# Adding one block of the weights to another by accumulating DMAs, with one more seven-multiplication row pair in fourteen of the MLP products

## The chip, the cores and the metric

The kernel runs on one core of one Trainium2 chip. The metric is the device time of one execution in microseconds (us); lower is better. Everything is float32 in and float32 out. Engines are named as in the profile: PE (TensorE, matmuls), DVE (VectorE), ACT (ScalarE), POOL (GpSimd) and SP (the queue that issues the weight loads).

## The reference

A decoder trunk of two layers over 256 tokens of width 2048. Layer 0 is a retention layer, layer 1 a latent attention (MLA) layer, and behind each stands an MLP with a squared ReLU. Nearly all of the work is in products of a 256-row activation with large weights:

```python
D_MODEL, SEQ, D_FF = 2048, 256, 4 * 2048

def sq_relu_mlp(h, w1, w2):
    return jnp.square(jax.nn.relu(h @ w1)) @ w2

for layer in range(2):
    if layer == 0:
        x = x + retention(rms_norm(x, norm_mix[0]), ret_w_in[0], ret_w_out[0], cos, sin)
    else:
        k_nope, k_pe, v = mla_shared_kv(rms_norm(x, kv_norm_in), ...)
        x = x + mla_attention(rms_norm(x, norm_mix[1]), ..., k_nope, k_pe, v, ...)
    x = x + sq_relu_mlp(rms_norm(x, norm_mlp[layer]), mlp_w1[layer], mlp_w2[layer])
```

`retention` is a projection (queries, keys, values, gate), a decayed causal attention per head, and an output projection; the MLP is two products of 256 x 2048 x 8192.

## The kernel before, in words

**One product.** Float32 accuracy is reached by splitting both factors into a high and a low part (`fp32r`). ACT casts the weights' high part (L185), DVE subtracts it to get the low part (L186), and each product of blocks is three matmuls: high by high (L356), high by low (L357), low by high (L358).

**Row pairs and column pairs.** `gemm_pair` (L333) computes 1024 columns of a product, one *pair*. It goes through the weights in *row pairs* of 256 rows. A row pair is one load of 1 MB (L285) into a tile `raw` of 128 x 2048, whose four blocks of 128 x 512 lie in the order B11, B12, B22, B21. `quad` (L282) works off one row pair. It comes in two kinds:

- An *eight* does the four block products of each of two token halves: 8 products, 24 matmuls of 512 columns. DVE has two splits of 1024 columns.
- A *seven* uses the Strassen-Winograd scheme: 7 products, 21 matmuls, on sums of activations (`more`, made by `with_sums`, L392) and sums of weights. Before the change, DVE makes the weights' sums by one addition of 1024 columns (L321, B12 added to B11 and B22 at once) and two of 512 (L324, L325). Its splits are 1024, 512, 1024 and 1024 columns. The products that need no sums come first, three of them or nine matmuls; then those on the third split (columns `b[:, 0:2]`), then those on the fourth.

Each pair has eight row pairs, numbered 0 to 7. Lists say which of them are sevens: `THREE = (3, 5, 7)`, `FOUR = (1, 3, 5, 7)`, and `HEAD = (2, 4, 6, 7)` for the retention part. In a pair with sevens there are further accumulators (`p1`, `p5`, `p6`, `p7`), which `pair_out` (L368) copies and combines into four pairs of partial results.

**Buffers.** `raw` has four buffers, the split halves `wh` and `wl` have five each. SP can load row pair k only when the last split of row pair k - 4 has read its buffer. ACT can cast only into a `wh` that PE has finished with. So the loads run about three row pairs ahead of DVE, and DVE runs less than a row pair ahead of PE.

**The MLP.** `mlp` (L784) goes in four groups of 2048 hidden columns. In a group there are two pairs of the first product, called u0 to u7 over the four groups, and two pairs of the second product, called d0 and d1 in each group. What follows a pair is done by ACT, DVE and PE while the row pairs of the next one run:

- after a u pair: `pair_out`, `summed` (L387), ReLU (L797), transposes on PE (L205), square (L806), the split of four tiles `hid`, and `with_sums` for those of them that a seven will use (L396 to L398, and the split of `hid_more`);
- after a d pair: `pair_out`, and `to_home` (L145), which adds eight 256 KB blocks to x in HBM by accumulating DMAs on POOL's queue (L150), two to each of four places, so that the second must wait for the first.

The last group's d pairs add to x in SBUF: `x_tiles` (L133) brings x back from HBM (L140), and `into_next` (L467) adds, stores and transposes it.

**Order.** Each engine runs its instructions in the order that a scheduler wrote when the kernel was built. `later`, `tick` and `need` decide where follow-up work enters; the scheduler then reorders by its own estimates. At run time only semaphores hold an instruction back, and POOL's accumulating DMAs are issued in POOL's order: one that waits holds up those behind it.

Of the kernel before, what the change touches and what calls it, by code (L numbers as in the profile page):

```python
# [11 lines left out]
F32 = mybir.dt.float32  # L12
# [4 lines left out]
ALU = mybir.AluOpType  # L17
# [3 lines left out]
P = 128  # L21
NT = 2
# [21 lines left out]
NB = 4  # L44
# [2 lines left out]
NOPE, ROPE, MV, KVR, QR = 128, 64, 128, 512, 1536  # L47
KV_NBS, Q_NB = (320, 256), 384
GROUPS = (4, 4, 4, 4)
THREE, FOUR, HEAD = (3, 5, 7), (1, 3, 5, 7), (2, 4, 6, 7)  # L50
PI = math.pi

G_MIX0, G_MLP0, G_KV, G_MIX1, G_MLP1 = 0, 16, 32, 48, 64
# [15 lines left out]
def yoco(ctx: ExitStack, tc: tile.TileContext, a):  # L69
    nc = tc.nc  # L70
# [20 lines left out]
    def act_tile(name, dtype=F32R):  # L91

        return pool.tile([P, 2, 2, S], dtype, tag="act", bufs=24, name=name)
# [8 lines left out]
    def run_first():  # L102
        i = min(range(len(queue)), key=lambda i: queue[i][:2])
        due, _, fn = queue.pop(i)
        fn()
# [6 lines left out]
    def need(items, n):  # L112
        while len(items) < n:
            run_first()
# [14 lines left out]
    dram = ctx.enter_context(tc.tile_pool(name="dr", bufs=1, space=bass.MemoryType.DRAM))  # L129
    x_home = [[dram.tile([P, 512], F32, name=f"xh_{t}_{b}") for b in range(NB)] for t in range(NT)]  # L130
    x = [[None] * NB for t in range(NT)]

    def x_tiles(name):  # L133


        def bring(b):
            both = act_tile(f"x_{name}{b}", F32)
            for t in range(NT):
                x[t][b] = both[:, t].rearrange("p i s -> p (i s)")
                nc.gpsimd.dma_start(x[t][b], x_home[t][b])  # L140

        for b in range(NB):
            later(2 * b, lambda b=b: bring(b))

    def to_home(c, p):  # L145

        for j in range(2):
            for t in range(NT):
                for part in c[t][j]:
                    nc.gpsimd.dma_start(x_home[t][2 * p + j], part, accum_op=ALU.add)  # L150

    def into_x(done, c, p):
        for j in range(2):
# [125 lines left out]

            stream(w, chunk0 + g, 2048, f"{name}{g}", use, (lambda: done(acc)) if g == n - 1 else None)  # L280

    def quad(w, chunk, x, mm, name):  # L282

        raw = pool.tile([P, 2048], F32, tag="raw", bufs=4, name=f"{name}_raw")
        nc.sync.dma_start(raw, w[chunk])  # L285
        v, more = x

        def a(t, k):
            return [v[:, k, i, t * P : (t + 1) * P] for i in range(2)]

        def s(n):
            return [more[:, n // 2, i, n % 2 * P : (n % 2 + 1) * P] for i in range(2)]

        b = raw.rearrange("p (i n) -> p i n", i=4)

        def parts(src, part):
            n = src.free_size() // 512
            wh, wl = (
                pool.tile([P, 2, 512], F32R, tag=f"w{i}", bufs=5, name=f"{name}_w{i}{part}")[:, :n] for i in "hl"
            )  # L300
            split(wh, wl, src)
            return [[i[:, j] for i in (wh, wl)] for j in range(n)]

        b11, b22 = parts(b[:, 0:3:2], 0)
        if more is None:
            mm("c11", a(0, 0), b11)
            mm("c21", a(1, 0), b11)
            mm("c12", a(0, 1), b22)
            mm("c22", a(1, 1), b22)
            b12, b21 = parts(b[:, 1:4:2], 1)  # L310
            mm("c12", a(0, 0), b12)
            mm("c22", a(1, 0), b12)
            mm("c11", a(0, 1), b21)
            mm("c21", a(1, 1), b21)
            return
        mm("p1", a(0, 0), b11)
        mm("c12", s(3), b22)
        (b21,) = parts(b[:, 3:4], 1)
        mm("c11", a(0, 1), b21)

        nc.vector.tensor_tensor(  # L321
            b[:, 0:2], b[:, 0:3:2], b[:, 1].unsqueeze(1).to_broadcast([P, 2, 512]), op=ALU.add
        )
        nc.vector.tensor_tensor(b[:, 2], b[:, 0], b[:, 2], op=ALU.add)  # L324
        nc.vector.tensor_tensor(b[:, 3], b[:, 2], b[:, 3], op=ALU.add)  # L325
        u1, u3 = parts(b[:, 0:2], 2)
        mm("p5", s(1), u1)
        mm("p7", s(0), u3)
        u2, u4 = parts(b[:, 2:4], 3)
        mm("p6", s(2), u2)  # L330
        mm("c21", a(1, 1), u4)

    def gemm_pair(w, chunk0, act, kinds, name, done):  # L333

        made = {}
        total, count = {}, {}
        for seven in kinds:
            for key in ("c11", "c12", "c21"):
                total[key] = total.get(key, 0) + (1 if seven else 2)
            for key in ("p1", "p5", "p6", "p7") if seven else ("c22", "c22"):  # L340
                total[key] = total.get(key, 0) + 1

        def get(key):
            if key not in made:
                if key in ("p6", "p7"):
                    both = two_banks(f"{name}_p67")
                    made["p6"], made["p7"] = both[:, 0], both[:, 1]
                else:
                    made[key] = bank("tp" if key[0] == "p" else "acc", [512], f"{name}_{key}")
            return made[key]  # L350

        def mm(key, lhs, rhs):
            dst, n = get(key), count.get(key, 0)
            count[key] = n + 1
            (ah, al), (bh, bl) = lhs, rhs
            nc.tensor.matmul(dst, ah, bh, start=n == 0, stop=False)  # L356
            nc.tensor.matmul(dst, ah, bl, start=False, stop=False)  # L357
            nc.tensor.matmul(dst, al, bh, start=False, stop=n == total[key] - 1)  # L358

        for i in range(len(kinds)):  # L360
            need(act, i + 1)
            v, more = act[i]
            quad(w, chunk0 + i, (v, more if kinds[i] else None), mm, f"{name}{i}")
            if i == len(kinds) - 1:
                queue.append((clock[0] + 1, -1, lambda: pair_out(made, name, done)))
            tick()
# [374 lines left out]
    for h in range(RH):  # L741
        qk, gate, v, s = [], [], [], []
        if h == 0:

            def gated(acc, gate=gate):
# [16 lines left out]
                lambda acc, v=v, s=s, gate=gate: ret_valued(acc, 0, s, v, gate),  # L762
# [14 lines left out]
        kinds = HEAD if h > 1 else HEAD[1:]  # L777
# [6 lines left out]
    def mlp(layer, act, r, done):  # L784
        w1, w2 = a[f"mlp_w1_{layer}"], a[f"mlp_w2_{layer}"]
        f0 = 0
        for gi, nf in enumerate(GROUPS):
            hid, blocks = [], []
            last = gi == len(GROUPS) - 1

            def up(c, p, hid=hid, blocks=blocks, last=last):

                need(r, NT)
                c = summed(c)
                for t in range(NT):
                    for i in range(2):
                        nc.scalar.activation(c[t][i], c[t][i], AF.Relu, scale=r[t])  # L797

                def turn(i):
                    for q in (2 * i, 2 * i + 1):  # L800
                        name = f"hid{layer}_{p}{q}"
                        tp = transposed(
                            lambda t, j: c[t][q // 2][:, (q % 2 * 2 + j) * P : (q % 2 * 2 + j + 1) * P], f"{name}_tp"
                        )
                        u = f2k([2, S], f"{name}_u")
                        nc.scalar.activation(u, tp, AF.Square)  # L806
                        v = act_tile(name)
                        split_act(v, u)
                        blocks.append((v, with_sums(u, name) if len(blocks) in (THREE if last else FOUR) else None))
                        hid.append(v)  # L810

                later(0, lambda: turn(0))
                later(1, lambda: turn(1))

            for p in range(f0 // 2, (f0 + nf) // 2):
                kinds = THREE[not (p or layer) :] if p % 2 or not p else FOUR
                gemm_pair(
                    w1, p * 8, act, [i in kinds for i in range(8)], f"u{layer}_{p}", lambda c, p=p, up=up: up(c, p)
                )
            if last:  # L820
                x_tiles(f"mlp{layer}")
            for p in range(2):
                if last and p and layer:
                    for b in (2, 3):
                        need(hid, 2 * nf)
                        gemm(
                            a["mlp_w2t"], (b - 2) * nf, hid, 4 * nf, 512, f"d{layer}_{gi}{b}",
                            lambda acc, b=b: done(b, acc),
                        )
                    continue  # L830

                def add(c, p=p, last=last):
                    into_x(done, c, p) if last else to_home(c, p)

                kinds = [i in (FOUR if p and not last else THREE) for i in range(2 * nf)]
                gemm_pair(w2, p * 32 + 2 * f0, blocks, kinds, f"d{layer}_{gi}{p}", add)
            f0 += nf

# [347 lines left out]
```

## Time and profile before

| what | value |
|---|---|
| times of three runs | 2477.63, 2477.06, 2475.72 us (median 2477.06) |
| the profiled execution's own time | 2474.51 us |
| its span, first to last instruction | 2472.7 us |
| granted TensorE clock | 1.000 |
| PE busy | 2455.6 us (99%) |
| DVE busy | 2167.4 us (88%) |
| ACT busy | 1606.1 us (65%) |
| POOL busy | 251.6 us (10%) |
| DMA moved | 521.04 MB, mean 211 GB/s |

Instructions overlap with the next one on their engine: a matmul of 512 columns is shown as 0.39 us, but the next one starts 0.23 us later. So the rate of an engine is read from the starts of consecutive rows of the timeline, and not from the durations. In a timeline row the first number is the start in us from the beginning of the span, the second the duration; a bracket at the end names the idle time before it and who ended it, and no bracket means that the engine went straight on.

### The profile page before, as it was taken

Reading aid. Unit: us, or ns where it says so; the run is one execution under the profiler, and the core shown is the slowest. Engines: PE = TensorE matmul, PEld = TensorE weight load, DVE = VectorE, ACT = ScalarE, POOL = GpSimd, SP = SyncE. Lnnn points to the kernel's source line nnn. Section 1 sums busy time; section 2 is a strip of 40 time slices with the busy share of each in tenths; the row PEclk is TensorE's granted clock in tenths of the full one; section 3 lists DMA queues with packets and bytes.
Section 4 is the critical chain, followed back from the end, with each engine's and each line's share of the span. In section 5 each row is a group of like instructions: output and inputs, shape, how many; then the busy total and the mean of one; then the engine's idle time right before and its main releaser. Section 6 shows DMA issues by size and latency. Waiting matters only on the chain.

```text
span 2472.7 us, 31711 instructions
## 1 busy us (share of the span) xinstructions
PE 2455.6 (99%) x11635; PEld 2060.0 (83%) x11635; DVE 2167.4 (88%) x2805; ACT 1606.1 (65%) x2253; POOL 251.6 (10%) x310
## 2 busy tenths in 40 slices
PE   9999999999999999999999999999999999999999
PEld 7888888888888888888888888998888888888887
DVE  7799899889899999999999967776689999999996
ACT  6566656556676667667666766676566666676663
POOL 7300011000010010110110101110000201101100
PEclk9999999999999999999999999999999999999999
DMA  9555567555564685684785564445545856857854
GB/s 328 211 174 205 196 205 234 199 192 201 198 236 182 209 262 216 213 254 172 246 263 196 192 228 168 153 155 179 199 174 199 261 212 209 268 203 225 266 192 153
DMA packets 93403, 521.04 MB, mean 211 GB/s; under 512 B 11072, under 2 KB 12224, under 8 KB 40000
## 3 DMA queue, kind: packets, MB, share of 16 engines
q1 hardware_dynamic: 71856, 472.83, 53.8%
q0 software_dynamic: 21248, 46.15, 8.5%
q8 instruction: 91, 1.49, 0.2%
q14 instruction: 64, 0.52, 0.1%
q10 hardware_dynamic: 144, 0.05, 0.0%
HBM read 479.14 MB, written 39.85 MB: 210 GB/s over the span
## 4 chain that ended last, share of the span: by engine, by line
PE 91%; DVE 4%; ACT 3%; issue 1%; POOL 1%; DMA 0%; SPq 0%; ACTq 0%; POOLq 0%; DVEq 0%
PE u_c L358 7%; PE u_c L356 7%; PE u_c L357 7%; PE d_c L357 6%; PE d_c L358 6%; PE d_c L356 6%; PE rk_acc L274 2%; PE rq_acc L274 2%; PE rp_c L356 2%; PE rp_c L357 2%; PE rp_c L358 2%; PE u_p L358 2%; PE u_p L356 2%; PE u_p L357 2%; PE d_p L356 2%; PE d_p L358 2%
## 5 line engine op out<-in xcount | busy, mean ns | idle before, releaser
L185 ACT CAST u_wh<-u_raw 128x1024 fp32r<-128x1024 f32 x362 | 347.9, 991 | 207.8 <-DVE u_raw L321 100.8
L185 ACT CAST d_wh<-d_raw 128x1024 fp32r<-128x1024 f32 x358 | 344.1, 993 | 202.5 <-DVE d_raw L321 93.9
L186 DVE TENSOR_TENSOR u_wl<-u_raw,u_wh 128x1024 fp32r<-128x1024 f32 x362 | 402.0, 1144 | 47.2 <-ACT u_wh L185 41.7
L186 DVE TENSOR_TENSOR d_wl<-d_raw,d_wh 128x1024 fp32r<-128x1024 f32 x358 | 397.8, 1146 | 40.1 <-ACT d_wh L185 35.5
L356 PE MATMUL u_c<-u_wh,n 128*128 128x512 f32 x706 | 276.4, 392 | 0.0
L357 PE MATMUL u_c<-u_wl,n 128*128 128x512 f32 x706 | 275.5, 390 | 0.0
L358 PE MATMUL u_c<-u_wh,n 128*128 128x512 f32 x706 | 274.9, 389 | 0.0
L356 PE MATMUL d_c<-d_wh,hid 128*128 128x512 f32 x654 | 256.0, 392 | 0.0
L357 PE MATMUL d_c<-d_wl,hid 128*128 128x512 f32 x654 | 255.4, 391 | 0.0
L358 PE MATMUL d_c<-d_wh,hid 128*128 128x512 f32 x654 | 254.6, 389 | 0.0
L185 ACT CAST rp_wh<-rp_raw 128x1024 fp32r<-128x1024 f32 (+1 forms) x166 | 160.7, 982 | 140.9 <-DVE rp_raw L321 64.9
L186 DVE TENSOR_TENSOR rp_wl<-rp_raw,rp_wh 128x1024 fp32r<-128x1024 f32 (+1 forms) x166 | 184.9, 1137 | 26.7 <-ACT rp_wh L185 24.4
L358 PEld LDWEIGHTS u_c<-u_wh,n 128*128 128x128 f32 x706 | 132.6, 188 | 27.4
L356 PEld LDWEIGHTS u_c<-u_wh,n 128*128 128x128 f32 x706 | 132.6, 188 | 26.9
L357 PEld LDWEIGHTS u_c<-u_wl,n 128*128 128x128 f32 x706 | 132.6, 188 | 26.7
L358 PEld LDWEIGHTS d_c<-d_wh,hid 128*128 128x128 f32 x654 | 122.8, 188 | 25.4
L356 PEld LDWEIGHTS d_c<-d_wh,hid 128*128 128x128 f32 x654 | 122.8, 188 | 25.2
L357 PEld LDWEIGHTS d_c<-d_wl,hid 128*128 128x128 f32 x654 | 122.9, 188 | 24.7
L150 POOL DMA_DIRECT2D xh<-d_c x48 | 41.6, 867 | 856.6 <-ACT d_c L373 854.7
L185 ACT CAST ro_wh<-ro_raw 128x1024 fp32r<-128x1024 f32 x88 | 85.7, 997 | 59.7 <-DVE ro_raw L321 25.7
L356 PE MATMUL rp_c<-rp_wh,a 128*128 128x512 f32 x286 | 111.9, 391 | 0.0
L357 PE MATMUL rp_c<-rp_wl,a 128*128 128x512 f32 x286 | 111.4, 390 | 0.2 <-DVE rp_wl L186 0.2
(465 smaller groups left out, 6075.6 us busy)
## 6 DMA issues: line engine op xcount, KB each, us to landing
u_raw<-in_mlp_w SPq DMA_DIRECT2D x128, 1024.0 KB, 5.2
d_raw<-in_mlp_w SPq DMA_DIRECT2D x120, 1024.0 KB, 4.9
rp_raw<-in_ret_w_gv SPq DMA_DIRECT2D x56, 1024.0 KB, 4.9
ro_raw<-in_ret_w_out SPq DMA_DIRECT2D x32, 1024.0 KB, 4.9
uq_raw<-in_mla_w_uq SPq DMA_DIRECT2D x24, 768.0 KB, 4.1
rq_raw<-in_ret_w_qk SPq DMA_DIRECT2D x16, 1024.0 KB, 5.0
rk_raw<-in_ret_w_qk SPq DMA_DIRECT2D x16, 1024.0 KB, 4.8
wo_raw<-in_mla_w_o SPq DMA_DIRECT2D x16, 1024.0 KB, 4.8
```

What stands on the lines that cost most here:

```text
L150: nc.gpsimd.dma_start(x_home[t][2 * p + j], part, accum_op=ALU.add)
L185: nc.scalar.copy(h, src)
L186: nc.vector.tensor_tensor(l, src, h.bitcast(F32), op=ALU.subtract)
L274: nc.tensor.matmul(acc[f], wh[:, cols], a.rearrange("p i s -> p (i s)"), start=k == 0, stop=k == nk - 1)
L356: nc.tensor.matmul(dst, ah, bh, start=n == 0, stop=False)
L357: nc.tensor.matmul(dst, ah, bl, start=False, stop=False)
L358: nc.tensor.matmul(dst, al, bh, start=False, stop=n == total[key] - 1)
```

## The change

1. `quad` no longer loads. A new function `block` loads a row pair and, for a seven, issues a DMA on POOL's queue that adds B11 to B12 inside `raw` (SBUF to SBUF, accumulating). `gemm_pair` calls it two row pairs ahead, so the accumulating DMA of row pair k stands in POOL's program ahead of the work on row pair k - 2.
2. DVE's three additions are then all of 512 columns. U1 is B11 + B12, which the DMA has made in the place of B12.
3. `FOUR` becomes (2, 3, 5, 7), and it is used in all u pairs but the first, and in both d pairs of every group but the last. The pairs that had three sevens and now have four are u1, u3, u5, u7 in both layers and the d0 of three groups in both layers: fourteen pairs.
4. `to_home` has a second place in HBM, `more_home`, for the second part of each block. The first write of a round is a plain one, later ones accumulate. `x_tiles` adds that place to x by a further accumulating DMA per block.

```diff
-THREE, FOUR, HEAD = (3, 5, 7), (1, 3, 5, 7), (2, 4, 6, 7)
+THREE, FOUR, HEAD = (3, 5, 7), (2, 3, 5, 7), (2, 4, 6, 7)
...
                 nc.gpsimd.dma_start(x[t][b], x_home[t][b])
+            for t in range(NT):
+                if (t, b) in has_more:
+                    nc.gpsimd.dma_start(x[t][b], more_home[t][b], accum_op=ALU.add)
+                    has_more.remove((t, b))
...
-                for part in c[t][j]:
-                    nc.gpsimd.dma_start(x_home[t][2 * p + j], part, accum_op=ALU.add)
+                b = 2 * p + j
+                part, more = c[t][j]
+                nc.gpsimd.dma_start(x_home[t][b], part, accum_op=ALU.add)
+                if (t, b) in has_more:
+                    nc.gpsimd.dma_start(more_home[t][b], more, accum_op=ALU.add)
+                else:
+                    nc.gpsimd.dma_start(more_home[t][b], more)
+                    has_more.add((t, b))
...
-    def quad(w, chunk, x, mm, name):
+    def block(w, chunk, seven, name):
 
         raw = pool.tile([P, 2048], F32, tag="raw", bufs=4, name=f"{name}_raw")
         nc.sync.dma_start(raw, w[chunk])
+        if seven:
+            nc.gpsimd.dma_start(raw[:, 512:1024], raw[:, 0:512], accum_op=ALU.add)
+        return raw
+
+    def quad(raw, x, mm, name):
...
-        nc.vector.tensor_tensor(
-            b[:, 0:2], b[:, 0:3:2], b[:, 1].unsqueeze(1).to_broadcast([P, 2, 512]), op=ALU.add
-        )
-        nc.vector.tensor_tensor(b[:, 2], b[:, 0], b[:, 2], op=ALU.add)
+        nc.vector.tensor_tensor(b[:, 2], b[:, 1], b[:, 2], op=ALU.add)
+        nc.vector.tensor_tensor(b[:, 0], b[:, 2], b[:, 0], op=ALU.subtract)
         nc.vector.tensor_tensor(b[:, 3], b[:, 2], b[:, 3], op=ALU.add)
-        u1, u3 = parts(b[:, 0:2], 2)
+        u3, u1 = parts(b[:, 0:2], 2)
...
+        raws = []
         for i in range(len(kinds)):
+            for k in range(len(raws), min(i + 3, len(kinds))):
+                raws.append(block(w, chunk0 + k, kinds[k], f"{name}{k}"))
             need(act, i + 1)
             v, more = act[i]
-            quad(w, chunk0 + i, (v, more if kinds[i] else None), mm, f"{name}{i}")
+            quad(raws[i], (v, more if kinds[i] else None), mm, f"{name}{i}")
...
-                kinds = THREE[not (p or layer) :] if p % 2 or not p else FOUR
+                kinds = FOUR if p else THREE[1 - layer :]
...
-                kinds = [i in (FOUR if p and not last else THREE) for i in range(2 * nf)]
+                kinds = [i in (THREE if last else FOUR) for i in range(2 * nf)]
```

More of the change, by code (lines that the diff above doesn't have):

```diff
@@ L131, in yoco @@
     x = [[None] * NB for t in range(NT)]
+    more_home = [[dram.tile([P, 512], F32, name=f"xm_{t}_{b}") for b in range(NB)] for t in range(NT)]
+    has_more = set()
     def x_tiles(name):
```

## The prediction

> **What bounds the kernel now.** I read the page's busy times and its chain first, then the windows of two stretches in the MLPs, then the timelines of DVE and PE where a pair with three sevens runs.
>
> ```profile
> PE 2455.6 (99%) x11635; PEld 2060.0 (83%) x11635; DVE 2167.4 (88%) x2805; ACT 1606.1 (65%) x2253; POOL 251.6 (10%) x310
> ...
> PE 91%; DVE 4%; ACT 3%; issue 1%; POOL 1%; DMA 0%; SPq 0%; ACTq 0%; POOLq 0%; DVEq 0%
> ```
>
> PE sets the end: 91% of the chain is PE. The mean hides how near the next engine is:
>
> ```profile
> core 0: us, PE busy (x) PEld busy (x) DVE busy (x) ACT busy (x) POOL busy (x), PEclk, DMA share, GB/s
> 938.00:978.00 40.00, 40.00 (x185) 32.97 (x184) 39.28 (x50) 28.20 (x38) 0.00 (x0) 1.00 0.53 195
> 1021.00:1103.00 82.00, 82.00 (x363) 67.83 (x362) 76.69 (x81) 50.95 (x61) 13.91 (x16) 1.00 0.86 257
> ```
>
> The first stretch is nearly all of pair u3 of layer 0, which has three sevens now and four after; the second is a d1 and the u4 behind it, which have four in both. In u3 DVE is busy 39.28 of 40 us: it has 0.7 us to give. In d1 and u4 it has 5.3 us in 82. So in the pairs that the change raises, DVE is a second bound right beneath PE. What PE would gain, and where DVE meets it, stands here (pair u5 of layer 0, row pair 3, PE):
>
> ```profile
> 1126.14 0.39 PE L356 MATMUL u_p<-u_wh,n 128*128 128x512 f32 x1
> ...
> 1128.18 0.39 PE L356 MATMUL u_p<-u_wh,n_more 128*128 128x512 f32 x1
> 1128.40 0.39 PE L357 MATMUL u_p<-u_wl,n_more 128*128 128x512 f32 x1
> ```
>
> From the first to the third row are ten matmuls in 2.26 us: one each 0.226 us, though each is shown as 0.39. The third row is the first matmul that reads a low part (`wl`) of row pair 3's third split. DVE's row for that split is in the next fence, at 1125.66.
>
> **Part 1, PE's gain.** Fourteen eights become sevens, in u1, u3, u5, u7 of both layers and the d0 of three groups of both layers. Each drops 3 of 24 matmuls: 42 x 0.227 = 9.5 us less, if PE never waits.
>
> **Part 2, what DVE must do in the raised pairs.** The new seven stands at row pair 2, ahead of the one at 3, and row pairs 0 to 3 are where DVE also carries the follow-up of the u pair before. DVE's timeline in u5 of layer 0 (row pair 2 is an eight here, row pair 3 a seven):
>
> ```profile
> 1107.57 2.36 DVE L186 TENSOR_TENSOR u_wl<-u_raw,u_wh 128x1024 fp32r<-128x1024 f32 x2 [0.21 <-ACT u_wh L185]
> ...
> 1119.79 0.69 DVE L186 TENSOR_TENSOR u_wl<-u_raw,u_wh 128x512 fp32r<-128x512 f32 x1
> 1120.40 0.29 DVE L398 TENSOR_TENSOR hid_sum<-hid_u,hid_sum 128x128 f32<-128x128 f32 x1
> 1120.60 1.23 DVE L321 TENSOR_TENSOR u_raw<-u_raw 128x1024 f32<-128x1024 f32 x1
> 1121.73 0.69 DVE L186 TENSOR_TENSOR hid_more<-hid_sum,hid_more 128x512 fp32r<-128x512 f32 x1
> ...
> 1125.66 2.35 DVE L186 TENSOR_TENSOR u_wl<-u_raw,u_wh 128x1024 fp32r<-128x1024 f32 x2
> 1127.93 0.68 DVE L186 TENSOR_TENSOR hid_more<-hid_sum,hid_more 128x512 fp32r<-128x512 f32 x1
> 1128.53 1.22 DVE L186 TENSOR_TENSOR u_wl<-u_raw,u_wh 128x1024 fp32r<-128x1024 f32 x1
> ...
> 1133.79 0.69 DVE L324 TENSOR_TENSOR u_raw<-u_raw 128x512 f32<-128x512 f32 x1
> 1134.52 0.69 DVE L325 TENSOR_TENSOR u_raw<-u_raw 128x512 f32<-128x512 f32 x1
> 1135.13 6.87 DVE L186 TENSOR_TENSOR u_wl<-u_raw,u_wh 128x1024 fp32r<-128x1024 f32 x6
> ```
>
> The bracket at 1107.57 is the last idle time before row pair 3: from there DVE runs without a gap, so whatever is added ahead of 1125.66 moves that split by as much. Step by step, from the starts of consecutive rows:
> - row pair 2's second split becomes 512 wide: 0.61 (1119.79 to 1120.40) instead of 1.14 (half of 1125.66 to 1127.93): -0.53;
> - its three additions of 512: 0.73 and 0.61 (1133.79, 1134.52, 1135.13) and once more 0.61: +1.95;
> - two more splits of 1024: +2.27;
> - row pair 3's first addition is 512 wide instead of 1024: 0.61 for 1.13 (1120.60 to 1121.73): -0.52;
> - in the changed program's order the `hid_more` split that runs at 1127.93 stands ahead of this split: +0.60.
>
> Sum +3.77 us. The first half of the split at 1125.66 ends at about 1125.66 + 1.22 = 1126.88, and PE reads it at 1128.40: a margin of 1.52. The changed program's PE order puts three matmuls on the high part, not one, ahead of the first on the low part: 2 x 0.226 = 0.45 more. PE's wait is then 3.77 less what PE itself comes sooner: it has 0.68 less to do in row pair 2. Measured against the program before, the end of the pair moves by 3.77 - 1.52 - 0.45 = **+1.80 us** (a wait of 2.48, less the 0.68 gained). Behind row pair 3 there is nothing to win it back, since PE goes straight on at its own rate.
>
> Twelve raised pairs are of this kind (u1, u3, u5 twice, six d0, which carry the same kind of follow-up): 12 x 1.80 = 21.6. The two u7 carry less, because the last group's d pairs have three sevens and so fewer sums of `hid`:
>
> ```profile
> 1293.04 2.35 DVE L186 TENSOR_TENSOR u_wl<-u_raw,u_wh 128x1024 fp32r<-128x1024 f32 x2
> ...
> 1297.07 0.39 PE L357 MATMUL u_p<-u_wl,n_more 128*128 128x512 f32 x1
> ```
>
> Their margin is 1297.07 - 1294.26 = 2.81, so 3.77 - 2.81 - 0.45 = 0.51 each, 1.0 for both. Together **+22.6**, with the 9.5 of part 1 already in it: both are measured as the end of the pair against before. Bounds: without the `hid_more` move each of the twelve is 1.20 (14.4); without the PE reordering 2.25 (27 + 2).
>
> **Part 3, the added transfers.** Every seven's `raw` now waits for its load, then for a DMA of 256 KB on POOL's queue. What such DMAs cost is seen only where they add to HBM:
>
> ```profile
> L150 POOL DMA_DIRECT2D xh<-d_c x48: 856/862/937, 852.7 to 2297.8; - x48
> ...
>   DMA xh<-d_c: 58.9, 9
> ...
> DMA to landing us min/median/max: 3.8/8.5/14.0
> ```
>
> Issue 0.86 us, landing 3.8 to 14.0 after it. I take 8.5, the median, as the upper middle and 3.8 as the low end, since source and target now lie in SBUF. The window is from the load's landing to DVE's first addition. It is least where x is being written, in d1 and in u2, u4, u6; row pair 7 of u4, layer 0:
>
> ```profile
> 1084.65 0.33 SPq L285 DMA_DIRECT2D u_raw<-in_mlp_w  x1
> ...
> DMA to landing us min/median/max: 8.3/8.3/8.3
> ...
> 1098.39 1.22 DVE L321 TENSOR_TENSOR u_raw<-u_raw 128x1024 f32<-128x1024 f32 x1
> ...
> 1100.97 1.22 DVE L186 TENSOR_TENSOR u_wl<-u_raw,u_wh 128x1024 fp32r<-128x1024 f32 x1
> ...
> 1105.27 0.39 PE L357 MATMUL u_p<-u_wl,n_more 128*128 128x512 f32 x1
> ```
>
> The load lands at 1093.0, the addition starts at 1098.39: 5.4 us, and the split ends 3.1 us (1105.27 - 1102.19) before PE reads it. So only an accumulate longer than 8.5 us costs anything there. Such places are the sevens at row pairs 5 and 7 of the twelve d1, u2, u4, u6 (windows 4.5 to 7.4 us): 24 in all. With a median of 8.5, half of them would be late, by little; I take 0.2 each, **+5 us**, with bounds of 0 and 0.8 x 24 = 19.
>
> The Trainium skill, "DMA: Bandwidth & Descriptors", section "Anatomy of one DMA — SWDGE (gpsimd) path", fits such a transfer as 2.0 us plus its bytes at 436 GB/s, an estimate of 2.6 us for 256 KB. By that nothing would be late here. No row of this trace is that short; the fastest is 3.8.
>
> In the raised pairs the loads come later, since SP waits for the split of four row pairs before (1125.66, which moves by 3.77):
>
> ```profile
> 1128.04 0.33 SPq L285 DMA_DIRECT2D u_raw<-in_mlp_w  x1
> ...
> DMA to landing us min/median/max: 5.0/5.0/5.0
> ...
> 1141.92 1.22 DVE L321 TENSOR_TENSOR u_raw<-u_raw 128x1024 f32<-128x1024 f32 x1
> ```
>
> Row pair 7 then lands at 1128.04 + 3.77 + 5.0 = 1136.8, and its addition comes at about 1143.7: a window of 6.9 and PE's slack of some 3 behind it. Nothing is counted.
>
> **Part 4, at nothing.** The narrower additions of the other sevens (0.52 each) are on DVE in pairs that PE bounds, so they move nothing. The second place in HBM takes away POOL's 58.9 us of waits for an earlier accumulate; POOL is 10% busy and nobody waits for it there. But an accumulate into `raw` stands behind these in POOL's order, so without that part it would have cost more. An accumulate that waits for its load in turn holds up what stands behind it on POOL: writes of x, for which nobody waits before the next round, and the next accumulate, whose load lands later anyway. The 24 or so further DMAs that bring x back lie beside PE work; were that cover gone, three stages x 8.5 = 25 us at most. The retention stages' 39 sevens have windows of 6 to 22 us. For all this together +-3.
>
> **Sum.** The profiled execution's own time is 2474.51; 2474.51 + 22.6 + 5 = 2502.1. The median of the runs is 2477.06, that is 2.55 more: **2504.7 us** (+1.1%). Its own range, with the first rival in it: 2491 (14.4, nothing late) to 2525 (29 and 19).
>
> **Rivals.**
> - *Nothing is late, the DVE lag alone.* Transfers of 4 to 5 us: 2504.7 - 5 = 2499.7. For it: everything stays in SBUF. Against: loads fill 0.86 of the DMA engines in the stretch of d1 and u4.
> - *Transfers late in most places.* If an accumulate takes 10 us among those loads, the 24 places are late by 10 - 8.5 = 1.5 each, 36, and fourteen others by 0.2, 3: 39 in place of 5, 2539. Decided by whether landings pass 8.5 us. The Trainium skill, "SBUF — State Buffer", section "SBUF: two separate sides", says more: a DMA issued from GpSimd is starved of descriptors while DVE runs certain two-port operations. As a mechanism of this kernel: DVE would come to each of the 118 MLP additions before the transfer had moved, and wait 0.86 + 8.5 less the slack of some 3, 6.3 x 118 = 743 us. Against it: the 48 rows above issue in 856 to 937 ns while DVE is 94% busy (76.69 of 82). I give it 1 in 100.
> - *Faster: the lag is covered.* If the scheduler's order lets DVE do the follow-up later than in before, the extra work ahead of row pair 3's third split is under 1.5 + 0.45 = 2 us, PE never waits, and the 9.5 stays: 2477.06 - 9.5 = 2467.5. For it: what is made of `hid` is read only by the d pair behind this one, so 1.8 us of it could stand further back. Against: the changed order has one `hid_more` split more ahead of that point, not fewer. It decides at 2 us of extra.
> - *Half of it.* Raised pairs move by 0.9 or less: a time near before, 2477.
> - *It does not do what it says:* the changed program's order shows 42 matmuls fewer and the transfers two row pairs ahead; no share.
>
> **Chances.** The forecast 0.46, nothing late 0.20, transfers late 0.14, faster 0.12, same 0.08. Of this kernel's times a difference of 0.2%, 5 us, is about what can be told from no change. Faster 0.12, same 0.08, slower 0.46 + 0.20 + 0.14 = 0.80. The range leaves out the faster case (0.12) and about half of the late one (0.07): from -0.2%, 2472, to 2532.
>
> **What the profile after would show.** Right: in raised pairs PE idles 2 to 3 us ahead of the third block of row pair 3, released by DVE's split of `raw` behind the new seven; DVE above 39.5 of 40 us there; PE's instruction count 42 lower (11593); the chain with more DVE than 4%. Part 3: DVE or ACT idle ahead of additions, put down to an accumulating DMA, mostly in d1 and u2, u4, u6. Wrong: PE busy without a gap in u3 and u5, with a pair 0.7 us shorter; or idle times put down to DMA in every pair; or DVE's order in row pairs 0 to 3 with the follow-up behind row pair 3.

## The result and the profile after

| | before | changed |
|---|---|---|
| median, us | 2476.49 | 2575.91 |
| lowest to highest of 4 runs | 2475.72 to 2477.63 | 2565.92 to 2578.97 |
| ratio, with its 95% interval | | 1.0394 [1.0365, 1.0423] |

The kernel became 99.4 us slower; 2504.7 was forecast, with 2532 as the upper end. The sign was right, the size missed by 71 us. The page of the changed kernel, busy times and chain:

```profile
PE 2490.2 (97%) x11593; PEld 2064.6 (80%) x11593; DVE 2136.8 (83%) x2875; ACT 1609.4 (62%) x2281; POOL 398.8 (15%) x491
...
PE 58%; DVE 16%; DMA 12%; issue 6%; ACT 5%; POOL 2%; ACTq 0%; SPq 0%; POOLq 0%; DVEq 0%
```

The 42 matmuls are gone (11593 for 11635), and yet PE is busy 34.6 us longer. The chain now has 12% of DMA, which was 0%, beside 16% of DVE, which was 4%. Two windows stand for the two kinds of loss: the raised pair u3, and the pair u4 beside writes of x (both of layer 0):

```profile
core 0: us, PE busy (x) PEld busy (x) DVE busy (x) ACT busy (x) POOL busy (x), PEclk, DMA share, GB/s
965.00:1012.30 47.30, 45.06 (x198) 36.13 (x197) 43.35 (x57) 32.70 (x45) 3.37 (x4) 0.96 0.63 201
...
1101.50:1148.60 47.10, 44.60 (x182) 35.74 (x181) 36.48 (x41) 25.40 (x32) 8.11 (x10) 0.93 0.90 267
```

u3 took 43.5 us before, u4 40.8; both take 47 now. The last column but two is new: a granted clock of 0.96 and 0.93, where it was 1.00.

Where the time went can be added up, since pairs follow each other on PE: a pair's length is the time from its first matmul to that of the next pair, and the differences to before are summed over four groups. *Raised*: the fourteen pairs with one more seven. *Beside writes*: the twelve d1 and u2, u4, u6. *Last d0*: the first d pair of each last group. *Retention*: its projections. All columns but the last come from one profiled execution of each kernel, in us against before; the kernels of the rows are those of the experiments below.

| kernel | raised | beside writes | last d0 | retention | other | sum | median of runs |
|---|---|---|---|---|---|---|---|
| changed | 40.3 | 29.0 | 15.6 | 17.8 | 1.5 | 104.2 | 2575.91 |
| e1_lists | 54.6 | 0.4 | 0.0 | 0.1 | 3.2 | 58.2 | 2534.31 |
| e2_transfers | 0.1 | 39.0 | 16.4 | 17.3 | 0.4 | 73.3 | 2537.40 |
| e3_no_writes | 41.6 | 1.8 | 0.0 | 14.5 | -0.5 | 57.3 | 2534.94 |
| e4_one_place | 40.5 | 95.7 | 0.0 | 19.8 | 0.1 | 156.0 | 2630.76 |
| e12_act_writes | 43.1 | 25.3 | 16.5 | 16.2 | 0.5 | 101.6 | 2578.54 |
| e13_act_later | 41.5 | 0.9 | 16.1 | 16.8 | 1.3 | 76.6 | 2551.97 |
| e14_one_read | 45.6 | 17.7 | 0.0 | 11.1 | 0.1 | 74.4 | 2549.83 |
| e6_quiet | 41.4 | 0.3 | 0.0 | -0.1 | 0.0 | 41.6 | 2517.25 |
| e7_quiet_three | 0.1 | -0.1 | 0.0 | 0.2 | 0.4 | 0.7 | 2476.24 |
| e11_fill | 28.9 | 0.5 | 0.0 | 0.3 | 1.6 | 31.3 | 2505.59 |
| e8_no_sums | 5.8 | 0.5 | 0.0 | 0.2 | 1.6 | 8.1 | 2482.59 |
| e5_quiet_late | 30.7 | 21.5 | 2.9 | 0.2 | 0.2 | 55.5 | 2530.94 |
| e9_even | 27.6 | 4.3 | 4.7 | 0.3 | 1.8 | 38.7 | 2514.93 |
| e10_pool_sums | 96.0 | 0.5 | 1.7 | 0.3 | 1.9 | 100.4 | 2573.45 |

One profiled execution can lie some us from the median of the runs (e2_transfers most, by 11): what lands late varies from one execution to the next. So only differences well above some 10 us are read from the columns with late transfers.

**The raised pairs.** DVE around row pair 3 of u5, layer 0, in the changed kernel:

```profile
1157.22 0.68 DVE L340 TENSOR_TENSOR u_raw<-u_raw 128x512 f32<-128x512 f32 x1
...
1169.08 0.68 DVE L199 TENSOR_TENSOR hid_more<-hid_sum,hid_more 128x512 fp32r<-128x512 f32 x1
1169.68 0.68 DVE L342 TENSOR_TENSOR u_raw<-u_raw 128x512 f32<-128x512 f32 x1
1170.32 3.58 DVE L199 TENSOR_TENSOR u_wl<-u_raw,u_wh 128x1024 fp32r<-128x1024 f32 x3
```

The third split starts at 1170.32, that is 21.72 us after the pair's first matmul (1148.59); before it was 17.89 (1125.66 - 1107.77). It moved by 3.83, and 3.77 was forecast. No bracket stands between 1157 and 1171: DVE has no gap. ACT does have gaps; the cast that PE needs next starts only when DVE's second addition is done:

```profile
1169.24 1.04 ACT L198 CAST u_wh<-u_raw 128x1024 fp32r<-128x1024 f32 x1 [0.76 <-DVE u_raw L341]
```

PE in the same place, and in u1 of layer 0:

```profile
1168.19 0.39 PE L375 MATMUL u_c<-u_wh,n 128*128 128x512 f32 x1
1170.33 0.73 PE L373 MATMUL u_p<-u_wh,n_more 128*128 128x512 f32 x2 [1.76 <-ACT u_wh L198]
1171.55 0.50 PE L373 MATMUL u_c<-u_wh,n 128*128 128x512 f32 x1 [0.48 <-ACT u_wh L198]
1171.89 0.40 PE L374 MATMUL u_p<-u_wl,n_more 128*128 128x512 f32 x1
1172.12 0.39 PE L375 MATMUL u_p<-u_wh,n_more 128*128 128x512 f32 x1
```
```profile
808.08 0.39 PE L375 MATMUL u_c<-u_wh,n 128*128 128x512 f32 x1
810.22 0.73 PE L373 MATMUL u_p<-u_wh,n_more 128*128 128x512 f32 x2 [1.75 <-ACT u_wh L198]
811.43 0.79 PE L373 MATMUL u_c<-u_wh,n 128*128 128x512 f32 x1 [0.49 <-ACT u_wh L198]
812.02 0.63 PE L374 MATMUL u_p<-u_wl,n_more 128*128 128x512 f32 x1
812.45 0.63 PE L375 MATMUL u_p<-u_wh,n_more 128*128 128x512 f32 x1
```

Both wait about 1.75 us and then 0.49. But in u5 the next matmuls come 0.23 us apart, in u1 0.43. Their clocks:

```profile
810.20:814.90 4.70, 4.20 (x10) 3.08 (x11) 4.70 (x6) 4.41 (x5) 0.00 (x0) 0.64 0.22 78
...
1170.30:1173.50 3.20, 2.68 (x11) 1.91 (x12) 3.20 (x4) 3.05 (x4) 0.00 (x0) 1.00 0.00 0
```

So u5 loses 2.22 us, u1 3.83: by these rows the difference is the clock (e11_fill, below, tries it). Of the twelve pairs with these waits, seven got the lower clock (3.67 to 3.88 us longer), five did not (2.13 to 2.55).

**Beside writes.** POOL and DVE in u4 of layer 0, row pair 5, and that one transfer's view:

```profile
1106.96 1.19 POOL L158 DMA_DIRECT2D xh<-d_c  x1
1107.51 1.53 POOL L160 DMA_DIRECT2D xm<-d_p  x1
1108.05 1.87 POOL L160 DMA_DIRECT2D xm<-d_u  x1
1108.59 2.21 POOL L160 DMA_DIRECT2D xm<-d_v  x1
1109.13 2.55 POOL L160 DMA_DIRECT2D xm<-d_p  x1
1114.51 0.86 POOL L300 DMA_DIRECT2D u_raw<-u_raw  x1 [2.84 <-DMA u_raw<-in_mlp_w]
```
```profile
DMA to landing us min/median/max: 14.3/14.3/14.3
```
```profile
1128.94 0.69 DVE L340 TENSOR_TENSOR u_raw<-u_raw 128x512 f32<-128x512 f32 x1 [4.11 <-DMA u_raw<-u_raw]
```

POOL issues the accumulate as soon as the load has landed, 0.6 us behind it. But five writes of x were issued just before, and it lands after 14.3 us; DVE stands 4.11 us for it, and PE behind DVE. Over the twelve pairs the accumulates at row pair 5 took 7.6 to 14.7 us, median 13.1; at row pair 7, with the writes done, 3.2 to 4.4.

The twelve pairs are not alike. In the first group of each layer the second place is still empty, so its writes are plain ones. The same row pair in u2 of layer 0, behind as many writes on the same queue:

```profile
936.61 0.89 POOL L300 DMA_DIRECT2D u_raw<-u_raw  x1 [3.70 <-DMA u_raw<-in_mlp_w]
...
DMA to landing us min/median/max: 7.9/7.9/7.9
...
946.88 0.69 DVE L340 TENSOR_TENSOR u_raw<-u_raw 128x512 f32<-128x512 f32 x1
```

It lands in time. The four pairs with plain writes (7.6 to 9.1 us at row pair 5) lose 0.1 us each; the eight in which all writes accumulate (12.2 to 14.7) lose 28.6 of the 29.0. In two of these, u4 of layer 0 and u6 of layer 1, the matmuls behind the wait come 0.43 us apart for a while: some 5.5 of the 28.6 us are the clock's and not the transfer's.

**The last d0.** The same two engines in the last group of layer 0:

```profile
1399.80 0.91 POOL L146 DMA_DIRECT2D x_mlp<-xm  x1 [5.64 <-DMA x_mlp<-xh]
1401.63 0.87 POOL L146 DMA_DIRECT2D x_mlp<-xm  x1 [0.92 <-DMA x_mlp<-xh]
1404.78 0.86 POOL L146 DMA_DIRECT2D x_mlp<-xm  x1 [2.28 <-DMA x_mlp<-xh]
1405.31 1.20 POOL L300 DMA_DIRECT2D d_raw<-d_raw  x1
```
```profile
1415.63 0.69 DVE L340 TENSOR_TENSOR d_raw<-d_raw 128x512 f32<-128x512 f32 x1 [8.60 <-DMA d_raw<-d_raw]
```

Each read of the second place waits on POOL for the read of the first into the same tile, and the accumulate into `raw` is issued only behind them, 5.6 us after its load had landed (1399.7). DVE waits 8.60 us. Before the change, DVE's first addition at this place had no wait:

```profile
1354.12 1.22 DVE L321 TENSOR_TENSOR d_raw<-d_raw 128x1024 f32<-128x1024 f32 x1
```

In the changed kernel the retention's last projection pair shows the same waits on POOL (it loses 9.9 us).

**Retention's first pair** lost 5.6 us to something else again, POOL's own computing:

```profile
113.44 0.29 POOL L541 TENSOR_SCALAR tm_rr<-tm_rr 128x128 f32<-128x128 f32 x1
114.04 1.84 POOL L300 DMA_DIRECT2D rp_raw<-rp_raw  x2 [0.31 <-issue]
```

The load had landed at 102.9; POOL was making tables without a gap from 92.8 to 113.7, and the accumulate stands behind them in its order. This is read from the trace; no run tries it apart. What is left of retention's 17.8 is mainly in the two pairs behind its own writes of x (1.0 and 2.8).

### The profile page after: what moved, and what is told of

The parts are those of the page before. It is cut to its first block, busy times and chain, and to the rows that moved or that the text cites. A ratio compares the mean times of both kernels' runs of the same rounds, so it can differ in the third digit from the quotient of the medians.

```text
span 2577.2 us, 32317 instructions
## 1 busy us (share of the span) xinstructions
PE 2490.2 (97%) x11593; PEld 2064.6 (80%) x11593; DVE 2136.8 (83%) x2875; ACT 1609.4 (62%) x2281; POOL 398.8 (15%) x491
## 4 chain that ended last, share of the span: by engine, by line
PE 58%; DVE 16%; DMA 12%; issue 6%; ACT 5%; POOL 2%; ACTq 0%; SPq 0%; POOLq 0%; DVEq 0%
PE u_c L373 4%; PE u_c L374 3%; PE u_c L375 3%; DMA d_raw<-d_raw 3%; DVE d_wl L199 3%; PE rq_acc L287 2%; DVE u_wl L199 2%; DMA u_raw<-u_raw 2%; PE d_c L373 2%; PE d_c L374 2%; PE d_c L375 2%; PE rk_acc L287 2%; PE ro_c L373 2%; PE ro_c L374 2%; PE ro_c L375 2%
## 5 line engine op out<-in xcount | busy, mean ns | idle before, releaser
L199 DVE TENSOR_TENSOR u_wl<-u_raw,u_wh 128x1024 fp32r<-128x1024 f32 x378 | 413.7, 1136 | 67.6 <-ACT u_wh L198 66.5
L373 PE MATMUL u_c<-u_wh,n 128*128 128x512 f32 x658 | 260.2, 395 | 3.4 <-ACT u_wh L198 3.4
L374 PE MATMUL u_c<-u_wl,n 128*128 128x512 f32 x658 | 257.7, 392 | 0.0
L375 PE MATMUL u_c<-u_wh,n 128*128 128x512 f32 x658 | 257.5, 391 | 0.0
L373 PE MATMUL d_c<-d_wh,hid 128*128 128x512 f32 x618 | 243.3, 394 | 2.9 <-ACT d_wh L198 2.9
L374 PE MATMUL d_c<-d_wl,hid 128*128 128x512 f32 x618 | 241.3, 390 | 0.0
L375 PE MATMUL d_c<-d_wh,hid 128*128 128x512 f32 x618 | 241.0, 390 | 0.0
L199 DVE TENSOR_TENSOR rp_wl<-rp_raw,rp_wh 128x1024 fp32r<-128x1024 f32 (+1 forms) x166 | 182.9, 1137 | 38.7 <-ACT rp_wh L198 37.8
L373 PEld LDWEIGHTS u_c<-u_wh,n 128*128 128x128 f32 x658 | 124.7, 189 | 32.2 <-ACT u_wh L198 6.8
L375 PEld LDWEIGHTS u_c<-u_wh,n 128*128 128x128 f32 x658 | 124.5, 189 | 26.2
L373 PEld LDWEIGHTS d_c<-d_wh,hid 128*128 128x128 f32 x618 | 116.5, 189 | 29.2 <-ACT d_wh L198 5.5
L375 PEld LDWEIGHTS d_c<-d_wh,hid 128*128 128x128 f32 x618 | 116.3, 188 | 24.5
L300 POOL DMA_DIRECT2D u_raw<-u_raw x61 | 52.7, 863 | 507.7 <-DVE u_raw L341 191.0
L300 POOL DMA_DIRECT2D d_raw<-d_raw x57 | 51.1, 897 | 462.5 <-DMA d_raw<-in_mlp_w 139.6
L199 DVE TENSOR_TENSOR ro_wl<-ro_raw,ro_wh 128x1024 fp32r<-128x1024 f32 x88 | 97.9, 1149 | 18.0 <-ACT ro_wh L198 17.5
```

Source lines behind the costliest of these rows:

```text
L199: nc.vector.tensor_tensor(l, src, h.bitcast(F32), op=ALU.subtract)
L300: nc.gpsimd.dma_start(raw[:, 512:1024], raw[:, 0:512], accum_op=ALU.add)
```

## The experiments

**Lists alone, transfers alone.** e1_lists is the kernel before with the three changed lines of the lists; e2_transfers is the changed kernel with these lines put back.

```diff
 # e2_transfers, against the changed kernel
-THREE, FOUR, HEAD = (3, 5, 7), (2, 3, 5, 7), (2, 4, 6, 7)
+THREE, FOUR, HEAD = (3, 5, 7), (1, 3, 5, 7), (2, 4, 6, 7)
-                kinds = FOUR if p else THREE[1 - layer :]
+                kinds = THREE[not (p or layer) :] if p % 2 or not p else FOUR
-                kinds = [i in (THREE if last else FOUR) for i in range(2 * nf)]
+                kinds = [i in (FOUR if p and not last else THREE) for i in range(2 * nf)]
```

> The kernel before with only the lists of the change: fourteen more sevens, the four at (2, 3, 5, 7), all additions by DVE, no added transfers, one place. In the changed kernel the raised pairs lost 40 us of the 104 (1.2 to 3.9 each). Theory (DVE's queue ahead of row pair 3 is the cause of that part): these pairs lose it here too, and about 0.9 more each, since DVE has 0.40 more of additions in row pair 2 and 0.52 more in row pair 3; nothing else loses. About 2477 + 40 + 14 x 0.9 = 2530 (2510 to 2550). Rival (the added transfers cause all of it): 2467 to 2477.

> The changed kernel with the lists of before: 42 matmuls more than the changed one, the sevens where they were, transfers and two places kept. Theory (two independent causes): the raised pairs' 40 us go, the 64 us of the places where an accumulating DMA lands late stay: about 2576 - 40 = 2536 (2520 to 2545). Rival (DVE's lag alone): 2477.

Measured: 2534.31 (ratio 1.0232 [1.0217, 1.0248]) and 2537.40 (1.0239 [1.0222, 1.0256]). The columns separate cleanly: e1_lists loses only in the raised pairs, e2_transfers everywhere but there. Neither part gains anything by itself. The transfers do help the raised pairs: 40.3 us with them, 54.6 without. (In e2_transfers the pairs beside writes have their sevens back at (1, 3, 5, 7) as well; that they lose 39.0 there and not 29.0 is mostly the d1 and u2 of layer 1 with plain writes beside them, which lose 8.1 us there.)

**Whose queue.** Five runs take the writes and reads of x apart. e3_no_writes drops `to_home` from the MLPs. e4_one_place puts the one place back. e12_act_writes sends the writes out on ACT's queue; e13_act_later does so by `later(2, ...)`. e14_one_read leaves the second place unread.

```diff
 # e12_act_writes, called in place of to_home by the MLPs
+    def by_act(c, p):
+        for j in range(2):
+            for t in range(NT):
+                b = 2 * p + j
+                nc.scalar.dma_start(x_home[t][b], c[t][j][0])
+                nc.scalar.dma_start(more_home[t][b], c[t][j][1])
+                has_more.add((t, b))
```

> The changed kernel without what the MLPs' d pairs write to x in HBM, except in each last group; x lacks those sums, and nothing else is left out. Theory (an accumulate into raw waits behind the writes of x in POOL's queue): the 28.6 us of d1 and u2, u4, u6 go, and part of the 15.6 us of each last group's first d pair, which has fewer reads of x ahead: 2576 - 29 to - 40, 2536 to 2547. Rival (the weight loads in the DMA engines make the accumulates late): 2565 to 2576.

> The changed kernel with one place in HBM for x: the second write of a block waits on POOL for the first again, and x is brought back by one read per block. Theory A (the bunch of eight writes and the accumulating reads is what makes the accumulates late): the last groups' 15.6 us and the retention's 10 us at its end go, and half of the 28.6: about 2576 - 40 = 2536. Theory B, the prediction's own (a write that waits on POOL holds up the accumulate behind it): the reads' 25 us go, but 24 places lose 3 us each more: about 2576 - 25 + 72 = 2620.

Measured: 2534.94 (1.0237 [1.0222, 1.0253]) and 2630.76 (1.0623 [1.0608, 1.0639]). Without the writes the twelve pairs lose 1.8 us, and the last d0 nothing, since the second place then holds nothing to be read back; that is why the time lies just below the expected range. The loads alone are not the cause: beside them the accumulates at row pair 5 landed after 3.2 to 7.6 us. With one place they lose 95.7: theory B, for this is what POOL then does in d1:

```profile
1097.42 0.85 POOL L158 DMA_DIRECT2D xh<-d_u  x1 [6.36 <-DMA xh<-d_c]
1097.96 1.19 POOL L158 DMA_DIRECT2D xh<-d_p  x1
1098.51 1.55 POOL L295 DMA_DIRECT2D d_raw<-d_raw  x1
```

A second write waits 6.36 us for the first, and the accumulate (load landed at 1089.9) stands behind it. The second place is what makes the transfers bearable at all: 95.7 against 29.0. The reads' part of the theory held for the last d0 (0.0) but not for retention in sum, which still loses 19.8, now in the two pairs behind its own writes (8.2 and 7.2).

> The changed kernel, but what the MLPs' d pairs (except each last group's) write to x goes out on ACT's queue as plain writes to the same two places; the same bytes move at the same time, only the last pair's part is kept in x. The reads back are as in the changed kernel. Theory (an accumulate into raw waits its turn behind the writes in POOL's own queue): the 28.6 us of d1 and u2, u4, u6 go, the last groups' 15.6 stay: 2576 - 29 = 2547 (2540 to 2552). Rival (the writes' traffic in the DMA engines, whichever queue it comes by): 2565 or more.

Measured: 2578.54 (1.0414 [1.0398, 1.0429]), no gain. But the accumulates at row pair 5 now take 4.2 to 7.6 us and lie ready 2.8 us or more ahead of DVE's addition. The loss is a different one, on ACT:

```profile
1066.42 3.46 ACT L206 CAST d_wh<-d_raw 128x1024 fp32r<-128x1024 f32 x4 [2.88 <-DVE d_p L408]
```

A write of a part that DVE makes had to wait for DVE, and ACT's casts behind it with it. The run had moved the wait, not removed it.

> As the kernel with the MLPs' writes of x on ACT's queue, but issued two row pairs later, so that ACT no longer waits for DVE's parts in front of its casts (that wait, 2.9 us in each d1 and u2, u4, u6, took the place of the accumulates' in the run before it). Theory (an accumulate into raw waits its turn behind the writes in POOL's own queue): the 29 us of these twelve pairs go, but for what ACT still waits for earlier writes: 2576 - 29 = 2547 (2545 to 2560). Rival (the writes' traffic in the DMA engines): 2570 or more, with accumulates that land later than 9 us after their issue.

> The changed kernel without the reads that add the second place to x when x is brought back; x lacks those parts, the writes stay. Theory (in the first d pair of each last group and in row pair 6 of the last projection pair of retention, the accumulate into raw stands in POOL's order behind reads of the second place, each of which waits for the read of the first): their 15.6 and 9.9 us go, everything else stays: 2576 - 25 = 2551 (2546 to 2556). Rival (the load traffic there is too dense for one more transfer): 2570 or more.

Measured: 2551.97 (1.0304 [1.0289, 1.0320]) and 2549.83 (1.0292 [1.0273, 1.0312]). With the same bytes written to HBM, but from another queue and by plain writes, the twelve pairs lose 0.9 us. The same accumulate as above lands after

```profile
DMA to landing us min/median/max: 7.1/7.1/7.1
```

and DVE comes to it 6.3 us later. So the cause is not the bytes written as such but the way the changed kernel writes them. Two things changed at once, though: ACT's writes are on another queue, and none of them accumulates. At row pair 5 the accumulates took 6.0 to 8.9 us here, 7.6 to 9.1 in the changed kernel where half of POOL's writes are plain, and 12.2 to 14.7 where all accumulate. How much is the queue's and how much the kind of write's was not tried apart. The Trainium skill, "DMA: Bandwidth & Descriptors", section "Queues, rings and completion order", says that a DMA engine takes turns between queues. That would let an accumulate on POOL's queue pass writes on ACT's; these runs agree with it, but do not show it by themselves.

Without the second reads the last d0 and the retention's last pair lose nothing (0.0 and 0.1): for these two the cause is shown. The rest of e14_one_read did not stay quite as it was: the pairs beside writes lost 17.7 instead of 29.0 and the raised ones 45.6 instead of 40.3, though nothing was changed for them, so part of the agreement in the time is luck.

**Where DVE limits.** e6_quiet has transfers only in the raised pairs, where no writes of x run; e7_quiet_three is the same with the lists of before. e5_quiet_late and e9_even move the sevens; e8_no_sums reads `hid` in place of its sums; e10_pool_sums gives sums to POOL.

```diff
 # e6_quiet, in gemm_pair and its callers; quad has both forms of the additions
-raws.append(block(w, chunk0 + k, kinds[k], f"{name}{k}"))
+raws.append(block(w, chunk0 + k, quiet and kinds[k], f"{name}{k}"))
 # u pairs: quiet = p % 2 == 1; d pairs: quiet = not p and not last
 # e5_quiet_late: FOUR = (3, 5, 6, 7); e9_even: FOUR = (2, 4, 6, 7)
```

> Accumulating DMAs only in the fourteen raised pairs, which have no writes of x beside them; DVE makes all additions elsewhere; one place in HBM; the lists of the change, sevens at (2, 3, 5, 7). Theory (two independent causes, the raised pairs' part being DVE's queue ahead of row pair 3): the raised pairs lose their 40 us as in the changed kernel, nothing else loses: 2476 + 40 = 2516 (2505 to 2520). Rival (the transfers play a part in the raised pairs, through the writes of x in front of them): under 2500.

> As the kernel with transfers only in the pairs without writes of x, but with the lists of before (three sevens there). Theory: the transfers cost nothing there and what they save on DVE gains nothing, since PE sets the pace: 2476, within 4. Rival (DVE already limits these pairs in before): some 0.5 us less in each of fourteen, 2469.

Measured: 2517.25 (1.0162 [1.0147, 1.0177]) and 2476.24 (0.9997 [0.9988, 1.0007]). Transfers in quiet pairs cost nothing and bring nothing; the raised pairs lose their 41 us with no writes of x anywhere near.

> As the kernel with transfers only in the raised pairs and sevens at (2, 3, 5, 7), but without the sums of hid and their splits: the products that need them read hid itself. That takes 2 x (0.33 + 0.20 + 0.20 + 0.60) = 2.7 us off DVE's follow-up at the front of each raised pair. Theory (DVE's queue): the 2.2 us that a raised pair loses without a drop of the clock go: 2476 - 5 = 2471 (2464 to 2480). Rival (ACT's casts, or the order of the matmuls, hold PE): over 2500.

Measured: 2482.59 (1.0023 [1.0014, 1.0032]): the raised pairs lose 5.8 us in all, 0.4 each. With 2.7 us off DVE nearly all of the loss goes, and the 11 us to what was expected are 0.8 in each of fourteen pairs, in which row pairs 2 and 3 still take 5.0 and 5.8 us where a seven that waits for nothing takes 4.76. The run also takes two casts of 128x512 off ACT. But in u5 of the changed kernel DVE had no gap ahead of row pair 3 and ACT had, and the cast that PE waits for was itself waiting for DVE (1169.24 above). So DVE's queue is the cause.

> As the kernel with transfers only in the raised pairs, but with sevens at (3, 5, 6, 7) in place of (2, 3, 5, 7). Theory A (place: the new seven stands where DVE still carries the follow-up of the pair before): the stall goes and PE's 0.68 us per raised pair stays: 2476 - 9.5 = 2467. Theory B (sum: DVE is busy 43.2 of 45.7 us in a raised pair of the changed kernel, wherever the seven stands, and PE would need 42.9): each raised pair becomes 0.5 to 1.7 us longer than before: 2483 to 2500.

> As the kernel with transfers only in the raised pairs, but all pairs of the MLPs with four sevens have them at (2, 4, 6, 7), those with three at (2, 4, 7), the first pair of layer 0 at (4, 7). A seven takes DVE about 6.6 us in a row of sevens, and PE 4.75; an eight takes DVE about 3.6 and PE 5.43. Theory (two sevens in a row are what DVE, less than one row pair ahead, cannot follow, and worst behind the follow-up): no stall at row pair 3, a small one of 0 to 0.3 us at row pair 7, PE's 0.68 us per raised pair stay: 2467 to 2475. Rival (the sum of DVE's work in a raised pair is what counts): each raised pair is 0.4 to 1 us longer than before: 2482 to 2490.

Measured: 2530.94 (1.0218 [1.0203, 1.0233]) and 2514.93 (1.0157 [1.0142, 1.0172]); both theories fell in both runs. At (3, 5, 6, 7) the odd u pairs lose only 0.7 to 0.9, but the d0 4.1 and the twelve pairs beside writes 1.8 each; in these twelve PE waits at row pair 7, the third seven in a row. At (2, 4, 6, 7) u1 is 0.4 to 0.5 shorter than before, the only gain seen; u3, u5 and u7 lose 1.4 to 1.6 and the d0 3 to 4. In a d0 three of the four sums of `hid` then come from the pair just before it, where two did: a likely reason, since where the sevens stand also decides when `hid` must be summed, but it was not tried apart. In none of the three places tried does a fourth seven pay.

> As the kernel with transfers only in the raised pairs and sevens at (2, 3, 5, 7), but POOL makes the sums of hid for the sevens, and the four sums of c in front of the ReLU after even u pairs: 1.5 us less on DVE in front of a d0, 3.9 in front of an odd u pair. Theory (DVE's queue): the odd u pairs turn from 2.2 to 3.8 us longer into 0.3 to 0.7 shorter than before, the d0 lose about 1 each: 2476 + 4 = 2480 (2472 to 2488). Rival (POOL is too slow for it: its 128x128 additions take 0.5 to 1.1 us, so one of 512 takes 1.8 to 4.3, and the accumulates wait behind them): over 2495.

Measured: 2573.45 (1.0385 [1.0368, 1.0402]), the rival's side. POOL's sums, u5 of layer 0:

```profile
1143.52 1.67 POOL L412 TENSOR_TENSOR u_c<-u_c,u_v 128x512 f32<-128x512 f32 x1 [1.77 <-DVE u_v L402]
1145.82 1.68 POOL L412 TENSOR_TENSOR u_c<-u_c,u_p 128x512 f32<-128x512 f32 x1 [0.63 <-DVE u_p L403]
```

Each is shown as 1.67 us where DVE's are shown as 0.68, and they wait for DVE between them. The raised pairs lose 96 us; that this is by what hangs on the sums coming later was not tried apart.

**The clock.** e11_fill is e6_quiet with PE kept busy in the wait of row pair 3:

```diff
+        if by_dma and name[-1] == "3":
+            fill("c11", a(0, 1)[0], b21[0])    # eight matmuls more
```

> As the kernel with transfers only in the raised pairs and sevens at (2, 3, 5, 7), but PE runs eight more matmuls (1.8 us) in row pair 3 of each raised pair, where it otherwise waits 1.75 us for a cast; they add a product of the same tiles once more, so the sums change. Theory (the pairs that lose 3.8 us instead of 2.2 do so because the granted clock drops after that wait): the wait is filled, the clock stays, all twelve such pairs lose 2.2 to 2.5: 2517 - 12 = 2505 (2500 to 2510). Rival (the 1.6 us are a second wait for DVE or ACT): 2517 or more.

Measured: 2505.59 (1.0117 [1.0101, 1.0134]), 11.7 us faster than e6_quiet though PE does 112 matmuls more. In u1 of layer 0:

```profile
791.48 1.97 PE L384 MATMUL u_c<-u_wh,n 128*128 128x512 f32 x8
793.39 0.73 PE L378 MATMUL u_p<-u_wh,n_more 128*128 128x512 f32 x2
794.61 0.50 PE L378 MATMUL u_c<-u_wh,n 128*128 128x512 f32 x1 [0.48 <-ACT u_wh L193]
794.95 0.40 PE L379 MATMUL u_p<-u_wl,n_more 128*128 128x512 f32 x1
795.18 0.39 PE L380 MATMUL u_p<-u_wh,n_more 128*128 128x512 f32 x1
```

The 1.75 us wait is filled, the matmuls behind come 0.23 us apart, and the twelve pairs lose 2.1 to 2.3 us each: no pair is left at 3.8. The clock's part in the raised pairs is shown.

## Why the prediction was wrong

**Part 1, PE's gain: right in count, used up by the waits.** 42 matmuls fewer, but in no raised pair did PE set the pace; the 0.68 us per pair are already taken off in the losses of part 2.

**Part 2, DVE's lag: right mechanism, mis-sized.** The split moved 3.83 for 3.77. Three things were missing from the 1.80 us per pair. First, a subtraction's end was set equal to its reader's start; 1171.54 (1170.32 + 1.22) and PE's 1171.89 lie 0.35 apart, which makes it 2.15, and the five pairs without a clock drop measured 2.13 to 2.55. Second, in the two u7 the split moved 4.50 and 4.25, not 3.77 (0.55 of it a wait of DVE for a cast of ACT), and they lost 1.4 and 1.2 in place of 0.51. Third and largest, the price of a wait on PE was taken as the wait alone. The clock that drops after it cost 1.4 to 1.6 us in each of seven pairs (3.67 to 3.88, less the 2.26 that the other five lost on average), 10.6 in all. With 12 x 0.35 = 4.2, 1.6 and 10.6 the 22.6 become 39.0; measured were 40.3, above the upper bound of 29. The Trainium skill, "TensorE: Matmul & The Clock Gate", section "Part 1: The HAM clock gate (the "warmup" mystery)", has the clock at half after an idle window of about 3.4 us that runs freely; by this, waits of 1.75 and 0.49 us should be safe. Here they were not in seven pairs of twelve. That the same waits drop the clock in some places and not in others would fit a window that runs freely; no run here tests it.

**Part 3, late accumulates: the failed step is the landing time.** 8.5 us, the median of writes that were spread out by waiting for each other, was taken for transfers that stand behind a bunch of them. It was 13.1 at row pair 5, and 29.0 us in place of 5 (bound 19). Where half of the bunch was plain writes (7.6 to 9.1), the 8.5 was about right and next to nothing was lost. Row pair 7, counted with row pair 5, cost nothing.

**Part 4, "at nothing": this failed most.** Retention and the last d0 lost 33.4 us against +-3. The estimate of "25 us at most" for the reads of x comes near the 25.5 that they cost (15.6 and 9.9) by luck: it missed whom the reads hold up, which is the accumulate into `raw` behind them in POOL's order. The prediction looked at the retention's windows and not at what else is on POOL there. That the change "would have cost more" without the second place was right: 66.7 us more in the pairs beside writes (95.7 - 29.0), 54.9 in the medians.

Of the rivals, late transfers in most places (2539, 0.14) came nearest: 62 of the 104 us stand in places with late transfers (29.0 + 15.6 + 17.8). Its mechanism was not the right one: it had the loads delay the accumulates, and without the writes of x the twelve pairs lost 1.8 us beside the same loads. Of the marks for "right", the count, the chain and the place of PE's wait were as said. Two were not: PE is released by ACT's cast rather than by DVE's split, because the third block's first matmul reads the high part, and that cast stands behind DVE's addition; and DVE is busy 43.35 of 47.30 us in u3, less than the 39.5 of 40 named, since the pair became longer.

## What to carry over

Before giving a transfer to a queue in order, list what else that queue carries in every stage, its own computing and its waits too: the transfer is issued behind all of these, however short it is by itself. Removing work from the bounding engine pays only where the next engine has room in that very stretch; here 0.68 us of PE cost 3.8 us of DVE. Price a wait on PE with the clock that may follow it.

## What was not expected of the hardware

- A wait of 1.75 us on PE, with one of 0.49 shortly behind it, was followed in 7 of 12 places by matmuls 0.43 us apart for some 3 us (granted clock 0.64), in 5 of 12 by none; eight more matmuls in the wait ended this and made the kernel 11.7 us faster (e11_fill against e6_quiet).
- An accumulate of 256 KB from SBUF to SBUF landed in 3.2 to 9.6 us in the raised pairs of the changed kernel, where no write stands ahead of it on POOL's queue, and in up to 14.7 behind writes that accumulate to HBM. DVE, busy without a gap for long stretches of the raised pairs, did not slow its issue: all 56 there took 0.84 to 0.86 us.
